# Inverting unit triangular matrices from 16x16 instead of 32x32 diagonal blocks, two chunks together, in a hybrid decoder layer

## The chip, the cores and the metric

The kernel runs on one core of one Trainium2 chip. A core has a matrix engine (PE, with its weight loads shown apart as PEld), a vector engine (DVE), an activation engine (ACT), a general engine (POOL) and an engine that issues transfers (SP). Each works through a queue of its own in a fixed order, and a transfer between on-chip memory and DRAM runs on DMA engines beside them. The metric is the device time of one execution, in microseconds (us).

## What is computed

One layer of a decoder over a prompt of 4096 tokens (width 1024), and one decoding step for 8 samples. The layer has a gated delta-rule half (4 heads of 128) and a sliding-window attention half (8 heads of 64); the change touches the first alone. Cut to that half, the reference is:

```python
h   = x * (1 + scale) + shift
p   = h @ w_in                              # one input projection
q, k, v = causal_conv(p[..., A_QKV])        # width 4, SiLU; q, k L2-normed
beta, g = sigmoid(p[..., BETA]), -exp(a_log) * softplus(p[..., DECAY] + dt_bias)

# per chunk of tokens and head, G = cumsum(g):
lower = eye + beta[:, None] * (k @ k.T) * exp(G_t - G_i)[t > i]
w_mat, u_tilde = solve(lower, [beta * exp(G) * k, beta * v])   # unit lower triangular
a_qk  = (q @ k.T) * exp(G_t - G_i)[t >= i]
# from chunk to chunk, S the state of a head:
u = u_tilde - w_mat @ S
o = (exp(G) * q) @ S + a_qk @ u
S = exp(G_last) * S + (exp(G_last - G) * k).T @ u
```

The solve needs the inverse of one unit triangular matrix per chunk and head. The kernel uses chunks of 128 tokens.

## The kernel before, in words

The program has two phases. Phase 1 (up to about 1270 us of the profile) runs the delta half; phase 2 runs the attention windows, gates and the output projection, and reads the weights that phase 1 split and stored for it. The change leaves phase 2's code alone.

Phase 1 goes over 16 supertiles of 256 tokens, two chunks `c` of 128 each, with 4 heads, so 8 triangular matrices of 128x128 per supertile. One supertile is written as:

- `front(s)`: the beta and decay products (tile `bd`, 32 small matmuls with weights `wbd`), a softplus by a polynomial in ten DVE operations (lines 101 to 108), the decays `g`, `g16`, `G`; projections into tile `pj` (12 blocks of 24 matmuls of 256 columns); the convolution on DVE (line 347); the matrices `k k^T` (tile `pga`), their decay masks (`tr<-g`), and U, the strictly triangular matrices, scaled by ACT at line 416 once a supertile; U is split into two 16-bit parts (U16). Inside it, `ahead()` loads and transposes the next supertile's x and makes its `hT`.
- `lanes(s, U)`, lines 437 to 466: the diagonal blocks of U, 32x32, are inverted by substitution on DVE. To lay them out by lanes, they go to DRAM (tile D1, 4 transfers at line 443) and come back replicated four times (LU, line 445, 512 KB). 31 steps of a multiplication (line 452) and an addition (line 454) follow, each on at most 8 x 31 columns. The result LV goes to DRAM (D2, line 456, 128 KB) and returns as diagonal blocks of VTd (4 transfers at line 461).
- `gdn_inv(c)`, once for each chunk, lines 470 to 513: on 4 matrices at a time, PE transposes VTd (line 487) and joins blocks 32 to 64 and 64 to 128. Each of the two levels is two groups of small matmuls (64 columns each), and between any two groups ACT (line 482) and DVE (line 483) take a result apart into two 16-bit halves.
- `gdn_c(s, c)`, once for each chunk: the recurrence of S with 128x128 products in 32-bit, and the output `oq`.

Beside this run the preparation of phase 2's weights (`prep`, `prep_s`), the gates' columns and, in steps, the decoding samples (`dec_a`). The framework's scheduler puts all instructions into one static queue per engine; a queue does not let later work pass one that waits. SP's queue issues all the transfers named here. Of the tiles in question U, U16, LU, LV, `vt16` and VTd have one buffer each.

Of the kernel before, what the change touches and what calls it, by code (L numbers as in the profile page):

```python
# [33 lines left out]
def body(ctx, tc, I, O, seq):  # L34
# [57 lines left out]
    D1 = [dr.tile([32, 1024], F32, name=f"D1_{i}") for i in range(2)]  # L92
    D2 = [dr.tile([32, 1024], F32, name=f"D2_{i}") for i in range(2)]
# [4 lines left out]
    def softplus_ops(t, x, out, shape, nm):  # L98
        """out = softplus(x) in SBUF tiles of one shape"""
        ab = t.tile(shape, F32, name=nm + "ab", bufs=2)  # L100
        dve.scalar_tensor_tensor(ab, x, -1.0, x, op0=ALU.mult, op1=ALU.max)
# [3 lines left out]
        dve.tensor_scalar(p, u, LOG1P[-1], None, op0=ALU.mult)  # L105
        for c in LOG1P[-2::-1]:
            dve.scalar_tensor_tensor(p, p, c, u, op0=ALU.add, op1=ALU.mult)
        dve.scalar_tensor_tensor(out, x, 0.0, p, op0=ALU.max, op1=ALU.add)

    # ================================================================ phase 1  # L110
    hpx = ctx.enter_context(ExitStack())
    hp = hpx.enter_context(tc.tile_pool(name="hp", bufs=2))
    with ExitStack() as p1:
# [40 lines left out]
        def raw():  # L154
            """a buffer for weights as they come, lent by the chunks' matrices"""
# [20 lines left out]
        # c^T, constants by channel  # L176
# [30 lines left out]
        # shift and scale: rows first, then by channel  # L207
# [24 lines left out]
        # ---- samples: h  # L232
# [9 lines left out]
        # ---- phase-1 weights  # L242
# [24 lines left out]
        XE = w1p.tile([128, 2, 4, 128], F16, name="XE")  # L267
        XZ = w1p.tile([128, 2, 4, 128], F16, name="XZ")
        V64 = w1p.tile([128, 2, 4, 64], F16, name="V64")
        VR = w1p.tile([128, 2, 4, 64], F16, name="VR")  # L270
        for t in (VTd, XE, XZ, V64, VR):
            pool.memset(t, 0.0)
# [19 lines left out]
        def front(s, hT, ahead):  # L292
            """projections, convolution, decays and the chunk's matrices"""
# [10 lines left out]
            be = sml.tile([128, 2, 4], F32, name="be")  # L304
# [5 lines left out]
            softplus_ops(sml, xd, g, [128, 2, 4], "sp")  # L310
            dve.tensor_mul(g, g, nega[:, None, :].to_broadcast([128, 2, 4]))
            dve.tensor_scalar(g, g, -30000.0, None, op0=ALU.max)
            g16 = sml.tile([128, 2, 8], F16, name="g16")
            gf = g.rearrange("p a b -> p (a b)")
            dve.tensor_copy(g16[:, 0], gf)
            dve.tensor_sub(g16[:, 1], gf, g16[:, 0])
            kqv = wk.tile([128, 8, 256], F32, name="kqv", bufs=2)
            vv = wf.tile([128, 4, 256], F32, name="vv", bufs=1)
            U = wk.tile([128, 8, 128], F32, name="U", bufs=1)
            U16 = wk.tile([128, 2, 8, 128], F16, name="U16", bufs=1)  # L320
# [35 lines left out]
            # keys  # L356
# [42 lines left out]
            # queries  # L399
# [15 lines left out]
            vt, vt16 = lanes(s, U)  # L415
# [10 lines left out]
            # values  # L426
# [8 lines left out]
            return kqv, G, sc, U16, Aqk, Kd, Vn, eGl, vt, vt16  # L435
# [984 lines left out]
```

## Time and profile before

| | us |
|---|---|
| median of 3 runs (2459.22 to 2463.24) | 2462.24 |
| span of the profiled execution | 2462.7 |
| PE busy | 2171.7 |
| DVE busy | 1942.7 |
| ACT busy | 1262.8 |
| POOL busy | 640.3 |

The profiled execution is 0.5 us above the median, so its durations can be set against the median as they are.

How the rows further down are to be read. A group row of the trace gives line, engine, operation, output tile, input tiles, shape and count, then total busy time and mean ns of one, then the engine's idle time just before, and what ended most of it; the view of one tile gives minimum, median and maximum in ns, and the times of the first and the last. A wait row gives the waiting engine, its output tile and line, what it waited for, and then total us, number of waits and the longest. A timeline row gives start and length in us; for SP the length is the time to issue.

A windows row gives the stretch and its length, then the busy us (and count) of PE, PEld, DVE, ACT and POOL, then the granted PE clock, the share of DMA engines busy and GB/s. Two kinds of stretch are told apart there. A *front stretch* runs from the scaling of U at line 416 to the first transposes of VTd at line 487, that is, through the transfers, the substitution and the transfers back. A *back stretch* runs from there to the next supertile's scaling at line 416. The recurrences lie partly in the one and partly in the other. Seven front stretches from 707.31 us on were summed, and eight back stretches from 677.36 us on. The mean of a sum row is over the stretches of that sum.

### The profile page before, as it was taken

To read this page: it belongs to the slowest core of one execution; us is meant where nothing else is said; L and a number is where in the kernel's file an instruction comes from. 1 tells how busy PE (TensorE), PEld (TensorE's weight loads), DVE (VectorE), ACT (ScalarE), POOL (GpSimd) and SP (SyncE) were. 2 spreads that over 40 slices of the span, in tenths; PEclk is the share of its full clock that TensorE was granted. 3 is DMA by queue.
4 is the path that set the end of the run, shared out by engine and by line. 5 is a ranking of instruction groups with operands and counts; after the bars stand their busy time and mean duration, and the time that the engine had idled before them with its cause. 6 is when DMAs were issued, how large, how long until landed. Compare 5 with 4: busy or idle time off the path is not lost. (4 is left out here: it accounts for less than half of the span.)

```text
span 2462.7 us, 49809 instructions
## 1 busy us (share of the span) xinstructions
PE 2171.7 (88%) x18596; PEld 1540.5 (63%) x18596; DVE 1942.7 (79%) x5348; ACT 1262.8 (51%) x3603; POOL 640.3 (26%) x669
## 2 busy tenths in 40 slices
PE   7988888878878888988899999999889888989986
PEld 4877777767766677777767677776445444444443
DVE  7678788767788877776776877776787789999997
ACT  6566555556557666545546656656323233333332
POOL 1122122202333311101100200000354555656552
PEclk8999999999899999999999999999999999999998
DMA  9232232322344221011314211110522222323231
GB/s 312 87 104 68 89 86 84 101 77 68 95 142 133 96 67 61 25 57 59 96 56 189 89 59 70 57 59 22 197 82 88 98 78 97 109 82 124 69 111 61
DMA packets 177409, 228.05 MB, mean 93 GB/s; under 512 B 65978, under 2 KB 120375, under 8 KB 171000
## 3 DMA queue, kind: packets, MB, share of 16 engines
q1 hardware_dynamic: 176696, 224.36, 28.0%
q8 instruction: 146, 2.39, 0.4%
q0 software_dynamic: 208, 0.37, 0.1%
q14 instruction: 95, 0.78, 0.1%
q10 hardware_dynamic: 264, 0.14, 0.0%
HBM read 149.88 MB, written 76.09 MB: 92 GB/s over the span
## 5 line engine op out<-in xcount | busy, mean ns | idle before, releaser
L41 PE MATMUL pj<-hT,w 128*128 128x256 f16 x4608 | 598.0, 281 | 5.9 <-ACT hT L287 2.8
L41 PEld LDWEIGHTS <-w 128*128 128x128 f16 x4800 | 459.8, 101 | 76.0 <-issue 15.7
L41 PEld LDWEIGHTS <-hT 128*128 128x128 f16 x2660 | 221.9, 99 | 146.1 <-issue 22.7
L41 PEld LDWEIGHTS <-S 128*128 128x128 f16 x1536 | 150.7, 98 | 182.2 <-issue 4.9
L41 PE MATMUL pj<-wq,hT 128*128 128x512 f16 x768 | 191.2, 381 | 1.9 <-DVE qt L826 1.9
L347 DVE SCALAR_TENSOR_TENSOR kqv<-u,cols,kqv 128x256 f32<-128x256 f32 x384 | 185.6, 490 | 7.2 <-ACT kqv L345 5.8
L452 DVE TENSOR_TENSOR lt<-LV,LU 128x60 f32<-128x60 f32 (+24 forms) x496 | 137.6, 277 | 65.4 <-DMA LU<-D 58.4
L1072 POOL TENSOR_TENSOR zt<-hT 128x512 f32<-128x512 f16 x32 | 43.2, 1351 | 496.6 <-DMA hT<-hD 496.6
L41 PE MATMUL pp<-wz,S 128*128 128x512 f16 x768 | 172.0, 382 | 0.1
L41 PE MATMUL pp<-wo,S 128*128 128x512 f16 x768 | 168.6, 379 | 1.0 <-DVE u L1107 1.0
L911 ACT ACTIVATE Sm<-Sm,nm 128x256 f32<-128x256 f32 (+1 forms) x256 | 125.5, 492 | 79.5 <-DVE nm L908 79.2
L41 PE MATMUL pp<-wz,hT 128*128 128x512 f16 x576 | 147.2, 405 | 0.0
L1072 POOL TENSOR_TENSOR zt<-zt,hT 128x512 f32<-128x512 f32 x112 | 142.8, 1280 | 6.3
L41 PE MATMUL pp<-wo,A 128*128 128x512 f16 x540 | 125.9, 389 | 11.7 <-DVE u L1105 8.9
L904 DVE CUSTOM_DVE_ANT_0 Sm<-pS,swam 128x256 f32<-128x256 f32 (+1 forms) x256 | 96.4, 415 | 38.2 <-PE tr L928 36.4
L332 POOL COPY u<-hist 128x6 f32<-128x6 f32 x96 | 24.9, 261 | 377.2 <-DVE kqv L347 104.8
L1241 POOL TENSOR_TENSOR u<-u,gateB 128x512 f32<-128x512 f32 x60 | 81.2, 1363 | 147.7 <-DVE u L1099 81.1
L454 DVE TENSOR_TENSOR LV<-LV,lt 128x60 f32<-128x60 f32 (+24 forms) x496 | 111.6, 225 | 7.1
L41 PE MATMUL pj<-wkv,hT 128*128 128x256 f16 x768 | 104.7, 273 | 0.4 <-ACT v L855 0.4
L41 PEld LDWEIGHTS <-A 128*128 128x128 f16 x540 | 53.9, 100 | 78.5 <-issue 16.8
L1135 POOL TENSOR_TENSOR x<-x,lnb 128x512 f32<-128x512 f32 (+1 forms) x62 | 84.9, 1380 | 67.5 <-ACT x L1134 67.5
L1066 ACT ACTIVATE S<-zt 128x512 f16<-128x512 f32 x64 | 40.0, 628 | 120.3 <-POOL zt L1072 120.3
(418 smaller groups left out, 5016.1 us busy)
## 6 DMA issues: line engine op xcount, KB each, us to landing
hT<-hD SPq DMA_DIRECT2D x32, 1024.0 KB
x<-in_x_prompt_dram SPq DMA_DIRECT2D x32, 512.0 KB
hD<-hT SPq DMA_DIRECT2D x16, 1024.0 KB
x<-in_x_prompt_dram SPq DMA_DIRECT2D x60, 256.0 KB
out_y_prompt_dram<-x SPq DMA_DIRECT2D x60, 256.0 KB
LU<-D SPq DMA_DIRECT2D x16, 512.0 KB
wS<-wt SPq DMA_DIRECT2D x16, 512.0 KB
oD<-oq SPq DMA_DIRECT2D x32, 256.0 KB
```

The lines of the kernel that those rows point to most:

```text
L41: pe.matmul(out, l, r, start=st, stop=sp_)
L332: pool.tensor_copy(u[:, :, 0:3], hist[:, b0:b0 + 2, :])
L347: dve.scalar_tensor_tensor(d, u[:, b2, j:j + 256], cwj(j, blk), d, op0=ALU.mult, op1=ALU.add)
L452: dve.tensor_mul(lt[:, j0:, 0:j], LV[:, j0:, j:j + 1].to_broadcast([128, n, j]), LU[:, None, 0:j, j].to_broadcast([128, n, j]))
L454: dve.tensor_add(LV[:, j0:, 0:j], LV[:, j0:, 0:j], lt[:, j0:, 0:j])
L904: dve.tensor_tensor_reduce(Sm[:, h, k0:256], pS[:, h2, k0:256], swam[:, k0:256], 0.125, -1e30, op0=ALU.add, op1=ALU.max, accum_out=mx[:, h ...
L911: act.activation(Sm[:, h, k0:256], Sm[:, h, k0:256], AF.Exp, bias=nm[:, h:h + 1], accum_out=sm_[:, h:h + 1])
L1066: act.activation(q[:, 0], src, AF.Copy)
L1072: pool.tensor_tensor(o, x, y, op=ALU.add if sgn > 0 else ALU.subtract)
L1135: (dve if last else pool).tensor_tensor(r[q][0:n], r[q][0:n], lnb[0:n, qs_], op=ALU.add)
L1241: (dve if last else pool).tensor_tensor(C, C, gateB[:, 512 * ch:512 * ch + 512], op=ALU.mult)
```

## The change

It alters four things in phase 1.

1. The diagonal blocks that DVE inverts are 16x16. U's blocks go out in 8 transfers and come back in 8; the replicated LU has 128 KB in two copies, LV 64 KB. There are 15 steps. LU and LV have two buffers, and LV's initial values are copied by POOL.
2. `gdn_inv` runs once for the 8 matrices of both chunks, and has a level 16 to 32 ahead of the two others. It has 144 products of 64 columns in place of 96 a supertile, 24 transposes in place of 16 (the last 8 of them 64x64), and splits of 512 columns. U16 has two buffers.
3. The decays are a function `decays(hT)`, called from `ahead`, so that those of supertile s+1 stand in the program inside supertile s; `be`, `g16` and `G` have three buffers.
4. Constants are loaded from ACT's queue and no longer from POOL's, `Sb` of the decoding step borrows a buffer, and the scratch memory for POOL's own transfers is made smaller.

```diff
-    D1 = [dr.tile([32, 1024], F32, name=f"D1_{i}") for i in range(2)]
+    D1 = [dr.tile([64, 256], F32, name=f"D1_{i}") for i in range(2)]
...
-        def front(s, hT, ahead):
+        def decays(hT):
             bd = tr_ps([128, 2, 16])
...
+            G = sml.tile([128, 4, 8], F32, name="G", bufs=3)
+            act.activation(G[:, 0], ps, AF.Exp)
+            act.activation(G[:, 1], ps, AF.Copy, scale=-1.0)
+            dve.tensor_scalar(G[:, 2], G[:, 0], -1.0, None, op0=ALU.mult)
+            return be, g16, G
+
+        def front(s, hT, dcy, ahead):
+            be, g16, G = dcy
...
-            for b in range(4):
-                bs = slice(32 * b, 32 * b + 32)
+            for b in range(8):
+                bs = slice(16 * b, 16 * b + 16)
                 sp.dma_start(d1v[b], U[bs, :, bs])
-            LU = w1p.tile([128, 32, 32], F32, name="LU", bufs=1)
-            sp.dma_start(LU.rearrange("p a b -> p (a b)"), d1[None].to_broadcast([4, 32, 1024]))
-            LV = w1p.tile([128, 8, 32], F32, name="LV", bufs=1)
-            dve.tensor_copy(LV.rearrange("p a b -> p (a b)"), lv0)
+            LU = w1p.tile([128, 16, 16], F32, name="LU", bufs=2)
+            sp.dma_start(LU.rearrange("p a b -> p (a b)"), d1[None].to_broadcast([2, 64, 256]))
+            LV = w1p.tile([128, 8, 16], F32, name="LV", bufs=2)
+            pool.tensor_copy(LV.rearrange("p a b -> p (a b)"), lv0)
...
-            for j in range(31, 0, -1):
-                j0 = j // 4
+            for j in range(15, 0, -1):
+                j0 = j // 2
...
-            d2w = d2.rearrange("l (j c i) -> c l j i", c=4, i=32)
+            d2w = d2.rearrange("l (j c i) -> c l j i", c=2, i=16)
             sp.dma_start(d2w, LV)
...
+            for c in range(2):
+                pb = pgi.tile([128, 4, 128], F32, name="pgi")
+                for h in range(4):
+                    pe.transpose(pb[:, h, :], vt[:, 4 * c + h, :], ident)
+                act.activation(V[:, 4 * c:4 * c + 4], pb, AF.Copy)
+            te = wk.tile([128, 2, 8, 64], F16, name="vt16", bufs=1)
+            sub([rows(te[:, z], 16) for z in range(2)], blocks(vt, 16, 0))
+            level(16, XF, te)
...
+            level(32, XE, te)
...
         def ahead(s):
             if s < NS:
-                nxt[0] = xt(s, load_x(s))
+                hT = xt(s, load_x(s))
+                nxt[:] = [hT, decays(hT)]
...
-            Vs = [gdn_inv(c, U16, vt, vt16) for c in range(2)]
+            V = gdn_inv(U16, vt)
             for c in range(2):
-                gdn_c(s, c, kqv, G, sc, Aqk, Kd, Vn, eGl, Vs[c])
+                gdn_c(s, c, kqv, G, sc, Aqk, Kd, Vn, eGl, V)
```

`level(b, XB, te)` is the new function for one level of 8 matrices: a split of V's off-diagonal half into `Vo`, 24 products with U16, a split into XB, 24 products with `Vo`, and the copies of the joined blocks into V, by ACT and DVE in turn. The scheduler's queues shift with it, at three places.

DVE, in the substitution of a supertile in the middle of phase 1, before; `spp` is the polynomial of the decays.

```order
L105 TENSOR_SCALAR spp<-spu 128x8
L452 TENSOR_TENSOR lt<-LV,LU 128x4x19
L107 SCALAR_TENSOR_TENSOR spp<-spp,spu 128x8
L454 TENSOR_TENSOR LV<-LV,lt 128x4x19
L107 SCALAR_TENSOR_TENSOR spp<-spp,spu 128x8
L452 TENSOR_TENSOR lt<-LV,LU 128x4x18
```

The same engine at the end of a substitution after; L360 is the convolution (L347 before).

```order
L360 SCALAR_TENSOR_TENSOR kqv<-u,cols,kqv 128x256
L460 TENSOR_TENSOR LV<-LV,lt 128x7x3
L360 SCALAR_TENSOR_TENSOR kqv<-u,cols,kqv 128x256
L458 TENSOR_TENSOR lt<-LV,LU 128x7x2
L360 SCALAR_TENSOR_TENSOR kqv<-u,cols,kqv 128x256
L460 TENSOR_TENSOR LV<-LV,lt 128x7x2
L458 TENSOR_TENSOR lt<-LV,LU 128x8
L460 TENSOR_TENSOR LV<-LV,lt 128x8
```

The decays' polynomial has left the substitution, whose steps stand among convolution operations alone.

DVE, in the last level of the inverse of one chunk, before; VR, V_368 (a buffer of V64) and XZ are written by splits of results.

```order
L483 TENSOR_TENSOR VR<-V,VR 64x256
L347 SCALAR_TENSOR_TENSOR vv<-u,cols,vv 128x256 x2
L483 TENSOR_TENSOR V_368<-pgi,V_368 64x256
L354 SCALAR_TENSOR_TENSOR kqv<-th,kqv 128x1024
L483 TENSOR_TENSOR XZ<-pgi,XZ 64x4x64
```

The same level after, for both chunks.

```order
L483 TENSOR_TENSOR VR<-V,VR 64x512
L483 TENSOR_TENSOR V_369<-pgi,V_369 64x512
L105 TENSOR_SCALAR spp<-spu 128x8
L107 SCALAR_TENSOR_TENSOR spp<-spp,spu 128x8
L367 SCALAR_TENSOR_TENSOR kqv<-th,kqv 128x1024
L107 SCALAR_TENSOR_TENSOR spp<-spp,spu 128x8
L360 SCALAR_TENSOR_TENSOR vv<-u,cols,vv 128x256
L107 SCALAR_TENSOR_TENSOR spp<-spp,spu 128x8
L360 SCALAR_TENSOR_TENSOR vv<-u,cols,vv 128x256
L483 TENSOR_TENSOR XZ<-pgi,XZ 64x8x64
```

Between the splits of V64 and XZ, where one other operation stood, there are seven; the polynomial is among them.

SP, the transfers of one supertile's lanes, before (`D_1_87` is D1, `D_1_89` is D2).

```order
L443 DMA D_1_87<-U 32x8x32 x3
L546 DMA oD<-oq 128x512
L443 DMA D_1_87<-U 32x8x32
L445 DMA LU<-D_1_87 128x1x1024
L546 DMA oD<-oq 128x512
L456 DMA D_1_89<-LV 4x256x32
L461 DMA VTd<-D_1_89 32x8x32 x4
```

The transfers of one supertile's lanes after.

```order
L572 DMA oD<-oq 128x512 x2
L449 DMA D_1_87<-U 16x8x16 x8
L451 DMA LU<-D_1_87 128x1x256
L462 DMA D_1_89<-LV 2x512x16
L467 DMA VTd<-D_1_89 16x8x16 x8
```

The outputs of the recurrence (`oq`) stand ahead of U's transfers and no longer among them.

## Rows read from the trace of the kernel before

**Rows 1.** Page, part 1: busy time, share, instructions of each engine, whole span.

```profile
PE 2171.7 (88%) x18596; PEld 1540.5 (63%) x18596; DVE 1942.7 (79%) x5348; ACT 1262.8 (51%) x3603; POOL 640.3 (26%) x669
```

**Rows 2.** ACT's scaling of U, line 416, once a supertile: first and last start.

```profile
L416 ACT ACTIVATE U<-U x16: 1042/1057/1058, 94.5 to 1212.4; 128x1024 f16<-128x1024 f32 x16
```

**Rows 3.** Windows, busy us: a front stretch, seven front summed, eight back summed.

```profile
931.60:978.20 46.60, 39.95 (x386) 34.91 (x385) 36.25 (x147) 27.65 (x99) 6.34 (x12) 1.00 0.16 40
sum 353.59, PE 285.62 PEld 248.14 DVE 266.75 ACT 198.75 POOL 76.74; mean PE 40.80 PEld 35.45 DVE 38.11 ACT 28.39 POOL 10.96
sum 181.45, PE 167.46 PEld 136.55 DVE 146.84 ACT 119.87 POOL 26.86; mean PE 20.93 PEld 17.07 DVE 18.36 ACT 14.98 POOL 3.36
```

**Rows 4.** Waits of PE, 115 to 1245 us: total us, times, longest.

```profile
PE tr L41 <- DVE g L315: 20.7, 7, 6.5
PE pgi L487 <- DMA VTd<-D: 16.3, 11, 2.7
```

**Rows 5.** Waits of DVE, the same stretch.

```profile
DVE lt L452 <- DMA LU<-D: 58.4, 15, 6.9
DVE LV L447 <- DMA D<-LV: 42.8, 13, 4.8
```

**Rows 6.** DVE groups by shape, 115 to 1245 us: busy us, mean ns.

```profile
L465 DVE TENSOR_TENSOR vt<-VTd,vt 128x512 f16<-128x512 f32 x15 | 10.4, 691 | 7.7 <-ACT vt L464 7.6
L483 DVE TENSOR_TENSOR XE<-pgi,XE 128x256 f16<-128x256 f32 x30 | 12.6, 421 | 1.2 <-ACT XE L482 0.8
L347 DVE SCALAR_TENSOR_TENSOR kqv<-u,cols,kqv 128x256 f32<-128x256 f32 x354 | 171.8, 491 | 6.4 <-ACT kqv L345 5.1
```

**Rows 7.** Tile LV: the substitution, ns minimum/median/maximum.

```profile
L452 DVE TENSOR_TENSOR lt<-LV,LU x496: 136/252/2237, 111.3 to 1245.8; 128x60 f32<-128x60 f32 x16, 128x28 f32<-128x28 f32 x12, 128x66 f32<-128x66 f32 x11, 128x48 f32<-128x48 f32 x10
L454 DVE TENSOR_TENSOR LV<-LV,lt x496: 170/214/2124, 111.8 to 1246.0; 128x60 f32<-128x60 f32 x16, 128x28 f32<-128x28 f32 x12, 128x66 f32<-128x66 f32 x11, 128x48 f32<-128x48 f32 x10
```

**Rows 8.** Timeline of SP in one supertile: start us, us it took to issue.

```profile
617.02 1.31 SPq L443 DMA_DIRECT2D D<-U  x3
619.59 0.96 SPq L443 DMA_DIRECT2D D<-U  x1
623.48 0.54 SPq L445 DMA_DIRECT2D LU<-D  x1
668.08 0.58 SPq L456 DMA_DIRECT2D D<-LV  x1
672.88 1.83 SPq L461 DMA_DIRECT2D VTd<-D  x4
```

**Rows 9.** Timeline of DVE, same supertile: first and last substitution steps.

```profile
632.72 0.21 DVE L452 TENSOR_TENSOR lt<-LV,LU 128x31 f32<-128x31 f32 x1 [4.70 <-DMA LU<-D]
666.34 0.21 DVE L452 TENSOR_TENSOR lt<-LV,LU 128x28 f32<-128x28 f32 x1
667.87 0.18 DVE L454 TENSOR_TENSOR LV<-LV,lt 128x8 f32<-128x8 f32 x1
```

**Rows 10.** Timeline of PE, two places: start us, us, count.

```profile
604.46 0.51 PE L41 MATMUL pgi<-vt,U 128*128 128x64 f16 x12
604.81 1.11 PE L41 MATMUL pga<-kqv 128*128 128x256 f32 x4
668.96 3.77 PE L41 MATMUL pj<-hT,w 128*128 128x256 f16 x33
677.36 0.63 PE L487 MATMUL pgi<-cf,VTd 128*128 128x128 f32 x4
...
1197.94 0.60 PE L487 MATMUL pgi<-cf,VTd 128*128 128x128 f32 x4
1205.10 0.22 PE L41 MATMUL pgi<-VR,XZ 128*128 128x64 f16 x2
1212.52 0.91 PE L41 MATMUL pgi<-S,kqv 128*128 128x128 f32 x6
1226.24 1.06 PE L41 MATMUL pgi<-ut,Aqk 128*128 128x128 f32 x8
```

More of the change, by code (lines that the diff above doesn't have):

```diff
@@ L266, in body @@
         VTd = w1p.tile([128, 8, 128], F32, name="VTd")
[L267 to L271, printed above, removed]
+        XF = w1p.tile([128, 2, 8, 128], F16, name="XF")
+        XE = w1p.tile([128, 2, 8, 128], F16, name="XE")
+        XZ = w1p.tile([128, 2, 8, 128], F16, name="XZ")
+        V64 = w1p.tile([128, 2, 8, 64], F16, name="V64")
+        VR = w1p.tile([128, 2, 8, 64], F16, name="VR")
+        for t in (VTd, XF, XE, XZ, V64, VR):
             pool.memset(t, 0.0)
@@ L483, in sub @@
                 dve.tensor_sub(dst[1], src, dst[0])
-            pb = pgi.tile([128, 4, 128], F32, name="pgi")
-            for h in range(4):
-                pe.transpose(pb[:, h, :], vt[:, m0 + h, :], ident)
-            act.activation(V, pb, AF.Copy)
-            vo = V.rearrange("p h (a b) -> p h a b", b=64)[:, :, :, 32:64]
-            sub([Vo[:, 0], Vo[:, 1]], vo)
-            px = pgi.tile([128, 4, 2, 32], F32, name="pgi")
-            for h in range(4):
-                mm3(px[:, h], lambda a: U16[:, a, m0 + h, :], lambda b: vt16[:, b, m0 + h])
@@ L502, in gdn_inv, with bank @@
[L502 to L511 removed]
+            def bank():
+                return pgi.tile([128, 8, 64], F32, name="pgi")
@@ new lines, in blocks, with rows, level @@
+            def blocks(t, b, o):
+                return t.rearrange("p m (a b) -> p (m a) b", b=2 * b)[:, :, o:o + b]
+            def rows(t, b):
+                return t.rearrange("p m (a b) -> p (m a) b", b=b)
+            def level(b, XB, te):
+                vo = wk.tile([128, 2, 8, 64], F16, name="Vo", bufs=1)
+                sub([rows(vo[:, z], b) for z in range(2)], blocks(V, b, b))
+                px = bank()
+                mm3(px, U16, te)
+                sub([blocks(XB[:, z], b, 0) for z in range(2)], rows(px, b))
+                pv = bank()
+                mm3(pv, XB, vo)
+                for n, a in enumerate(range(64 // b)):
+                    r0 = 2 * b * a
+                    dst, src = V[r0:r0 + b, :, r0 + b:r0 + 2 * b], pv[r0:r0 + b, :, a * b:a * b + b]
+                    if n % 2 == 0:
+                        act.activation(dst, src, AF.Copy)
+                    else:
+                        dve.tensor_copy(dst, src)
@@ new lines, in gdn_inv @@
+            for c in range(2):
+                cs = slice(4 * c, 4 * c + 4)
+                pt = pgi.tile([128, 4, 128], F32, name="pgi")
+                for h in range(4):
+                    pe.transpose(pt[:, h, :], V[:, 4 * c + h, :], ident)
+                sub([rows(te[:, z, cs], 32) for z in range(2)], blocks(pt, 32, 0))
+            level(32, XE, te)
+            sub([VR[64:128, z] for z in range(2)], V[64:128, :, 64:128])
+            pt = bank()
+            for m in range(8):
+                pe.transpose(pt[0:64, m, :], V[0:64, m, 0:64], ident[0:64, 0:64])
@@ L512, in gdn_inv @@
+            sub([V64[0:64, z] for z in range(2)], pt[0:64])
+            p2 = bank()
+            mm3(p2, U16, V64)
+            sub([XZ[64:128, z, :, 0:64] for z in range(2)], p2[64:128])
+            p3 = bank()
+            mm3(p3, XZ, VR)
             act.activation(V[0:64, :, 64:128], p3[0:64], AF.Copy)
@@ L532, in gdn_c @@
             for h in range(4):
[L533 removed]
+                mm(pw[:, h, :], V[:, m0 + h, :], r[:, h, :])
             ut = wk.tile([128, 4, 128], F32, name="ut", bufs=1)
@@ L743, in body @@
         load_bd()
+        nxt.append(decays(nxt[0]))
         for g in (4, 5, 6, 7):
```

108 lines of the change are left out of this document (40 added, 68 removed).

## The prediction

> **What bounds the kernel now.** I read the engines' busy times first [rows 1]: PE is busy for 2171.7 of 2462.7 us, so over the whole span little is left to win by filling PE. But the change touches phase 1 alone, and there the share has to be read by stretch. The scaling of U comes once a supertile, 16 times from 94.5 to 1212.4 us [rows 2], so a supertile takes 1117.9 / 15 = 74.5 us. The windows then tell where PE is idle [rows 3]. A front stretch (U out, LU in, substitution, LV out, VTd in) lasts 353.59 / 7 = 50.5 us, and PE works 40.8 of them: 9.7 idle. A back stretch lasts 181.45 / 8 = 22.7 us, and PE works 20.9: 1.8 idle. A period of these is 73.2 us (the early supertiles, with gates and decoding beside them, are longer), PE's own work in it 61.7 us, its idle time 11.5.
>
> What ends the idle time [rows 4]: PE waits 20.7 us in all for the decays' g, 16.3 for VTd. DVE waits 58.4 us for LU and 42.8 for the old LV to leave before it may be filled anew [rows 5]; since DVE's queue lets nothing pass, these waits hold up what PE reads next too. So the front stretch is set by the chain of transfers and substitution, and PE's 40.8 us of work there, nearly as long, covers most of it. Shortening that chain pays only as far as PE's work in the stretch is shortened or moved.
>
> **The chain, step by step, in one heavy supertile** [rows 8, 9, 10]. U's first transfer 617.02 to LU's issue 623.48: 6.46 (the four issues take some .45 each; from the last one's end at 620.55, landing takes 2.9). LU to the first step 632.72: 9.24. Steps until 668.05: 35.3, with much other DVE work between. LV's issue to VTd's first 672.88: 4.8. Four issues 1.83. Landing until the first transpose at 677.36: 2.65. Sum 60.3 in this long one.
>
> **The change, part 1: transfers and substitution.** Eight issues in place of four, at .44 (1.31 / 3): 3.5; landing 2.9 as before. LU has 128 KB in place of 512: no row shows it, it lies between 2.9 (a landing with little data) and 9.24; I take 4.8, the time of the 128 KB that LV now takes, the nearest row in size. Of the 31 steps the 15 narrowest stay. The four last pairs took 668.05 - 666.34 = 1.71 [rows 9], .43 each, so 15 take 6.5; the medians of .252 and .214 [rows 7] would give 7.0. The queue after the change has one split and six convolution operations between them: 0.69 + 6 x 0.49 = 3.6 [rows 6]. I take 10, between 6.5 and, by the heavy supertile's pace, 35.3 x 15 / 31 = 17. LV's way out: 4.8, although it has half the bytes. Eight issues of VTd at .46: 3.7. Landing 2.65. Front chain: 3.5 + 2.9 + 4.8 + 10 + 4.8 + 3.7 + 2.65 = **32.4 us**, bounds 27 (LU 2.9, steps 6.5) and 44 (9.24, 17). LV's first values are copied by POOL into a second buffer, so the 42.8 us of DVE waiting go; I cost the copy at nothing, since POOL is busy 26% [rows 1] and the buffer is free a supertile ahead. Uncovered it costs under 1 us a supertile.
>
> **Part 2: what PE does meanwhile.** The chain is shorter only if PE's work leaves the front, and the new order moves it: of some 230 projections in a front stretch 52 go to the back, with all 32 beta and decay products, some 11 transposes of x, and 24 products of the recurrence (32-bit). Prices [rows 10]: projection 3.77 / 33 = .114, so 5.9; 32-bit products 0.60 / 4 = .15, so 1.7 and 3.6; the 32 small ones at some .025, 0.8. Sum 12.0: PE has 40.8 - 12.0 = 28.8 us of work in a chain of 32.4, so the chain still ends last, by 3.6.
>
> **Part 3: the back stretch.** 12.0 us arrive. New work: 48 more products of 64 columns at (604.81 - 604.46) / 12 = .029, 1.4 us, and 8 more transposes at .15 or less, 1.2 us. At the back's present ratio of length to work, 22.7 / 20.9 = 1.085: 22.7 + 14.6 x 1.085 = 38.5. Against it stands the chain through the inverse, which is now one for both chunks: one chunk's took 1205.10 - 1197.94 = 7.2 with two levels [rows 10], so three levels of both some 7.2 x 2 x 1.5 = 21.6, and both recurrences behind it 1212.52 to 1227.3, 14.8. That is 36.4, just under PE's 38.5. A split is twice as wide (512 columns took .691, 256 .421 [rows 6]). I add 0.7, one such split that PE finds no other work for: **39.2 us**, bounds 36 and 44.
>
> **Part 4: decays ahead, loads.** PE's 20.7 us for g, 1.3 a supertile [rows 4], lie in the idle time that the front sum replaces, so nothing is added for them: DVE's polynomial now stands beside the inverse's splits, where the back sum's bounds hold it. The constants' loads, the decoding step's borrowed buffer and phase 2: no change, within 3 us in all.
>
> **Sum.** 32.4 + 39.2 = 71.6 for 73.2, -1.6 us a supertile, times 16: -26. From 2462.7 that is **2437 us**.
>
> **Rivals.** *R1, PE is the bound.* The two stretches run into each other (two buffers of LU, LV and U16 allow it), and nothing but PE's work counts: 61.7 + 2.6 = 64.3, with 2 us of its idle time left 66.3; -6.9 x 16 = -110, **2352 us**. For it: VTd's waits are 16.3 us in all, 1 us a supertile, so PE mostly finds other work [rows 4]. Against it: U has one buffer, and PE's waits in the back grow with the longer chain.
>
> *R2, slower: the inverse's hand-offs set the back.* The joined inverse has no second chunk to run beside it. It has some 15 hand-offs from PE to ACT and DVE and back, and each split stands behind convolution operations of .49 and polynomial steps. At 0.5 us more for each hand-off the chain is 36.4 + 7.5 = 43.9, the period 32.4 + 43.9 = 76.3, +3.1 x 16 = +50: **2512 us**. It decides from a back of 73.2 - 32.4 = 40.8, or 0.3 us a hand-off. For it: seven DVE operations stand between two splits of the chain that one parted before. Against it: today the splits wait hardly at all, 1.2 us in 30 [rows 6].
>
> *R3, slower: the passes through DRAM do not get shorter.* LU and LV have half as many outer pieces (two, not four). If each piece goes at a pace of its own, fewer bytes don't help as far. Taking 2.65 as the fixed part, LU's pieces of 128 KB took 9.24 - 2.65 = 6.6, so 64 KB take 3.3, and LU 5.95. LV's pieces had 256 rows in 4.8 - 2.65 = 2.15; they now have 512 half as long, so up to 4.3, and the pass 6.95. The front is 1.15 + 2.15 longer, 35.7, the period 74.9, +1.7 x 16 = +27: **2490 us**. For it: the 512 KB of LU take only twice as long as the 128 KB of LV, so time goes not by bytes alone [rows 8, 9]. Against it: 2.65 as the fixed time is an estimate from one landing of 32 KB transfers.
>
> The Trainium skill speaks for R3, and against this change: "DMA: Bandwidth & Descriptors", section Rules for kernel authors, says that an outermost dimension of fewer than 16, a leading broadcast of c copies above all, confines a transfer to at most c engines; LU and LV would go from 4 engines to 2. No row shows which engines a transfer used, so the trace neither confirms nor denies it; by it the sum would be R3's.
>
> **How the numbers follow.** Forecast .50, R1 .17, R3 .18, R2 .15. The measurement tells about 0.2% from no change, here 5 us. Of the forecast's share .43 lies below 2457, .05 within and .02 above (a substitution at 17 us would do it). R1 is faster; of R3 .03 and of R2 .02 lie within, the rest above. Faster .60, same .10, slower .30. The range reaches from near R1 to beyond R3, 2360 to 2500: it leaves out half of R1 and most of R2's upper half, .18.
>
> **What would show it.** The front window at some 32 us (33.6 or longer with its LU above 5.5 would be R3), with PE at 29 us of work; DVE's waits for LU near a half of 58.4, and those for the old LV gone; 15 pairs of steps in 10 us. The back window at 39 with PE idle under 3; idle over 5 there, released by splits, would be R2. Period of U's scaling 73 in the mean for 74.5. I am wrong if PE's waits within the inverse exceed 4 us a supertile, if work said to move stays in the front, or if phase 2, which no line of the change touches, moves by more than 3 us.

## The result, and the profile after

The changed kernel takes 2497.48 us (median of 4 runs, 2492.07 to 2505.32) beside 2462.74 of the kernel before in the same session: ratio 1.0136, 95% interval 1.0112 to 1.0159, so it is 1.4% slower, 35 us. The forecast was 2437. Of the rivals, R3 named 2490.

The busy times of the whole span, the row that answers [rows 1]:

```profile
PE 2198.5 (88%) x19492; PEld 1570.6 (63%) x19492; DVE 1860.5 (75%) x4788; ACT 1284.4 (51%) x3619; POOL 625.7 (25%) x681
```

PE works 26.8 us longer, DVE 82 us less. The scaling of U, the row that answers [rows 2], as the view of the tile gives it (in the code this line is ACT's copy of U into its 16-bit part U16, in both kernels; as a mark for the stretches it serves as well):

```profile
L422 ACT ACTIVATE U<-U x16: 1046/1057/1088, 97.1 to 1237.1; 128x1024 f16<-128x1024 f32 x16
```

From first to last it is 1140.0 us for 1117.9: 22.1 of the 35 us. Of these the twelve periods in the middle make 17.4, the first two 16.4, and the last is 11.7 shorter; why those at the two ends differ so was not looked into. 2.7 lie ahead of the first scaling and the rest behind the last. The first projection with `wq` (phase 2) starts 33.7 us later than before, and the end of the span is 33.7 later. Phase 2 itself has not moved.

Up to the copy `hr<-tr` near the end of phase 1 (line 777 before, 805 after), one window of each kernel (length, PE busy, PEld, DVE, ACT, POOL, granted clock, DMA share, GB/s), before:

```profile
0.00:1228.20 1228.20, 1042.23 (x9935) 881.97 (x9936) 945.08 (x3009) 732.23 (x2270) 240.60 (x349) 0.94 0.31 95
```

and after:

```profile
0.00:1259.90 1259.90, 1064.17 (x10769) 909.97 (x10770) 877.95 (x2500) 754.65 (x2293) 230.69 (x362) 0.94 0.29 86
```

Phase 1 is 31.7 us longer up to there; PE is busy 21.9 of them and idle 9.8. So the time that DVE gave back (67 us in this stretch) bought PE nothing.

To set stretch against stretch, the same twelve periods were taken in every kernel, from the third scaling of U to the fifteenth (the prediction had seven front and eight back stretches of mixed supertiles, which [rows 3] shows). Fronts first, backs second, summed; the kernel before:

```profile
sum 626.07, PE 509.06 PEld 444.13 DVE 479.97 ACT 363.61 POOL 157.68; mean PE 42.42 PEld 37.01 DVE 40.00 ACT 30.30 POOL 13.14
sum 280.91, PE 263.65 PEld 216.19 DVE 224.00 ACT 180.02 POOL 31.19; mean PE 21.97 PEld 18.02 DVE 18.67 ACT 15.00 POOL 2.60
```

The changed kernel:

```profile
sum 430.67, PE 324.71 PEld 282.17 DVE 274.35 ACT 220.21 POOL 81.16; mean PE 27.06 PEld 23.51 DVE 22.86 ACT 18.35 POOL 6.76
sum 493.70, PE 467.96 PEld 405.84 DVE 370.78 ACT 342.77 POOL 100.79; mean PE 39.00 PEld 33.82 DVE 30.90 ACT 28.56 POOL 8.40
```

A period has 75.6 us before and 77.0 after. The front fell from 52.2 to 35.9 us, as meant, and PE's work there from 42.4 to 27.1; its idle time in the front was 9.8 and is 8.8. The back grew from 23.4 to 41.1, with 39.0 of work. PE's waits, the rows that answer [rows 4]:

```profile
PE tr L393 <- DVE kqv L367: 77.0, 14, 8.1
PE pgi L515 <- DMA VTd<-D: 25.0, 8, 5.4
PE tr L437 <- DVE vv L367: 10.7, 5, 8.9
```

The waits for g are gone. The longest now has 77.0 us, in 14 waits, where it had 13.9 us in 4: the transposes of the keys wait for the last step of the keys' SiLU on DVE (L367, L354 before). One supertile in the middle shows why. SP (start, time to issue):

```profile
640.46 4.32 SPq L449 DMA_DIRECT2D D<-U  x8
646.32 0.50 SPq L451 DMA_DIRECT2D LU<-D  x1
664.72 0.52 SPq L462 DMA_DIRECT2D D<-LV  x1
672.31 3.64 SPq L467 DMA_DIRECT2D VTd<-D  x8
```

DVE, first and last step of the substitution and what follows:

```profile
651.46 0.18 DVE L458 TENSOR_TENSOR lt<-LV,LU 128x15 f32<-128x15 f32 x1 [1.49 <-DMA LU<-D]
664.52 0.17 DVE L460 TENSOR_TENSOR LV<-LV,lt 128x8 f32<-128x8 f32 x1
665.84 2.31 DVE L367 SCALAR_TENSOR_TENSOR kqv<-th,kqv 128x1024 f32<-128x1024 f32 x1 [1.15 <-ACT th L366]
```

PE, up to the first transposes of VTd:

```profile
651.51 9.88 PE L41 MATMUL pj<-hT,w 128*128 128x256 f16 x89
661.79 0.28 PE L41 MATMUL pga<-c,g 128*128 128x128 f16 x2
668.20 1.12 PE L393 MATMUL tr<-cf,kqv 128*128 128x128 f32 x4 [6.14 <-DVE kqv L367]
...
677.68 1.04 PE L515 MATMUL pgi<-cf,VTd 128*128 128x128 f32 x8
```

LU took 5.14 us to its first step, the 15 steps 13.2, with 12 convolution operations and a piece of the decoding step between them, and the pass of LV, from its issue to VTd's first, 7.59. PE has done its projections and masks by 662.1 and then waits 6.14 us for L367, which stands behind the substitution in DVE's queue; it does the little work that stands next and is at VTd's transposes at 677.68.

DVE stands still in the same place, before its half of the split of VTd:

```profile
678.03 0.69 DVE L483 TENSOR_TENSOR vt<-VTd,vt 128x512 f16<-128x512 f32 x1 [7.51 <-ACT vt L482]
```

It waits 7.51 us, until VTd has landed and ACT has made the other half, and nothing in its queue can pass. From 95 to 1263 us these waits have 9.4 us in the kernel before and 79.0 in the changed one:

```profile
DVE vt L465 <- ACT vt L464: 9.4, 10, 2.4
DVE vt L483 <- ACT vt L482: 79.0, 13, 8.6
```

DVE's waits for LU did fall as the prediction had it, from 58.4 to 30.6 us, and those for the old LV are gone.

Over the 16 supertiles the medians are (each from the rows of SP, DVE and PE as above):

| | before | forecast | after |
|---|---|---|---|
| issuing U's transfers | 2.7 | 3.5 | 3.8 |
| landing, to LU's issue | 2.1 | 2.9 | 1.3 |
| LU's issue to first step | 9.4 | 4.8 | 5.6 |
| first step to last | 27.8 | 10 | 11.8 |
| LV's pass through DRAM | 4.77 | 4.8 | 7.54 |
| issuing VTd's transfers | 1.8 | 3.7 | 3.6 |
| landing, to the transposes | 1.6 | 2.65 | 1.7 |
| sum | 50.2 | 32.4 | 35.4 |

LV's pass has half the bytes of before and takes 2.8 us longer, in every supertile (7.52 to 7.70, but for the first). R3 had priced the front at 35.7, and the prediction's sign for it, a front of 33.6 us or longer with LU above 5.5, is met.

### The profile page after: what moved, and what is told of

Read it like the earlier page. It is cut to its first block, busy times and chain, and to the rows that moved or that the text cites. A ratio compares the mean times of both kernels' runs of the same rounds, so it can differ in the third digit from the quotient of the medians.

```text
span 2496.4 us, 51161 instructions
## 1 busy us (share of the span) xinstructions
PE 2198.5 (88%) x19492; PEld 1570.6 (63%) x19492; DVE 1860.5 (75%) x4788; ACT 1284.4 (51%) x3619; POOL 625.7 (25%) x681
## 5 line engine op out<-in xcount | busy, mean ns | idle before, releaser
L41 PEld LDWEIGHTS <-w 128*128 128x128 f16 x4800 | 451.3, 100 | 77.0 <-issue 17.0
L41 PEld LDWEIGHTS <-hT 128*128 128x128 f16 x2660 | 228.4, 99 | 164.6 <-issue 19.7
L360 DVE SCALAR_TENSOR_TENSOR kqv<-u,cols,kqv 128x256 f32<-128x256 f32 x384 | 179.0, 493 | 28.6 <-ACT kqv L358 27.1
L41 PE MATMUL pj<-wq,hT 128*128 128x512 f16 x768 | 182.6, 382 | 0.0
L41 PE MATMUL pp<-wo,A 128*128 128x512 f16 x540 | 127.9, 393 | 12.7 <-DVE u L1133 9.4
L932 DVE CUSTOM_DVE_ANT_0 Sm<-pS,swam 128x256 f32<-128x256 f32 (+1 forms) x256 | 95.0, 415 | 33.7 <-PE tr L956 33.2
L41 PEld LDWEIGHTS <-A 128*128 128x128 f16 x540 | 54.2, 101 | 81.6 <-issue 19.6
L393 PE MATMUL tr<-cf,kqv 128*128 128x128 f32 x128 | 28.1, 350 | 81.9 <-DVE kqv L367 77.0
L1162 ACT ACTIVATE x<-x,rs 128x512 f32<-128x512 f32 (+1 forms) x62 | 42.8, 715 | 106.5 <-DVE x L1161 103.4
```

The source lines that it names most:

```text
L41: pe.matmul(out, l, r, start=st, stop=sp_)
L360: dve.scalar_tensor_tensor(d, u[:, b2, j:j + 256], cwj(j, blk), d, op0=ALU.mult, op1=ALU.add)
L393: pe.transpose(pk[:, h, :], kqv[:, 4 + h, c * 128:(c + 1) * 128], ident)
L932: dve.tensor_tensor_reduce(Sm[:, h, k0:256], pS[:, h2, k0:256], swam[:, k0:256], 0.125, -1e30, op0=ALU.add, op1=ALU.max, accum_out=mx[:, h ...
L1162: act.activation(r[q][0:n], r[q][0:n], AF.Copy, scale=rs[0:n, 1:2])
```

## The experiments

Two theories stood first. *Pieces*: the time goes into LV's and LU's passes, which are slow because the transfers have two outer pieces. *Order*: the queues' order is what counts; PE waits for the keys' SiLU behind the substitution, and LV's pass lies beside that. A third, *work*: what was added is the third level.

Every kernel's queues are ordered anew when it is built, so unless it is said otherwise two kernels differ in their order too. In the sessions of these runs the kernel before took 2462.7 to 2468.2 us, so where two runs of different sessions are compared, the difference of their ratios to the kernel before, taken of 2462.7 us, is given beside that of their times.

**LV's pass alone (a1_lv).** Two transfers, each with the 64 lanes outermost:

```diff
-            sp.dma_start(d2w, LV)
+            for z in range(2):
+                sp.dma_start(d2w[z], LV[64 * z:64 * z + 64])
```

> The changed kernel, but LV is written to DRAM by two transfers of 64 partitions each, with the 64 lanes as their outermost dimension, in place of one with an outermost dimension of two. Theory 'pieces' (the pass of LV through DRAM is slow since the write has two outer pieces, and this pass ends the front stretch): the pass, from LV's issue to VTd's first issue, falls from 7.5 us to some 3.5; the front stretch falls from 35.5 to 32; the kernel from 2497 to about 2450. Theory 'order' (PE's idle time in the front is its wait for the keys' SiLU, 77 us in all, which stands behind the substitution on DVE, and the pass is beside it): the pass may fall, but only PE's waits for VTd, 25 us in all, can go: 2475 to 2497.

Measured: 2435.88 us, ratio 0.9883 (0.9861 to 0.9904) to the kernel before. 62 us are back. SP of one supertile:

```profile
623.67 0.54 SPq L451 DMA_DIRECT2D LU<-D  x1
642.41 1.21 SPq L463 DMA_DIRECT2D D<-LV  x2
645.20 4.21 SPq L468 DMA_DIRECT2D VTd<-D  x8
```

The pass is 2.79 us from first issue to VTd, 2.81 in the median for 7.54. 4.73 us less in each of 16 supertiles are 76 us, and 62 came. PE's wait that 'order' took for the cause is as large as ever:

```profile
PE tr L393 <- DVE kqv L367: 74.2, 14, 8.7
```

but PE's waits for VTd, 25 us, are gone, and DVE's waits at VTd's split fell from 79.0 to 44.0 us:

```profile
DVE vt L484 <- ACT vt L483: 44.0, 15, 6.6
```

The two theories parted at 2475; the time is far below it. So the pass does not lie beside the chain, as 'order' had it, and PE's list of waits alone had shown too little: a VTd that comes late also holds DVE's queue, and with it all that stands behind. PE has as much work in a front as in the changed kernel (27.0 us for 27.1) and is idle 6.0 us there for 8.8. Two things stay open: the queues are ordered anew, so not each of the 62 us is shown to be the transfer's, and whether this write is faster by being two transfers or by having its lanes outermost was not told apart.

**LU too (a3_lvlu)**, by two transfers of 64 partitions (`for z in range(2): sp.dma_start(LU[64 * z:64 * z + 64]..., d1)`):

> As a1_lv, and LU too is read by two transfers of 64 partitions, one for each copy. Theory 'pieces': LU falls from 5.6 us to about 4, LV's pass from 7.5 to 3.5, the front to 30.5, the kernel to about 2430. Theory 'order': the substitution starts 1.6 us earlier and PE's waits for the keys' SiLU fall by that, 25 us in all, on top of at most 25 for VTd: 2450 to 2480.

Measured: 2391.6 us, 0.97 (0.9678 to 0.9722). LU's time is 4.4 for 5.6; the waits for L367 fall from 74 to 52 us. More than either theory gave.

**LU by its outermost dimension alone (a7_outer).** One transfer, as in the changed kernel, same bytes and rows; the lanes are numbered so that a lane's two copies are neighbours:

```diff
-            sp.dma_start(LU.rearrange("p a b -> p (a b)"), d1[None].to_broadcast([2, 64, 256]))
+            sp.dma_start(LU.rearrange("p a b -> p (a b)"), d1[:, None].to_broadcast([64, 2, 256]))
...
-                sp.dma_start(d2w[z], LV[64 * z:64 * z + 64])
+                sp.dma_start(d2w[z], LV[z::2])
...
-            lane[p, jj, 2 * jj + p // 64] = 1.0
+            lane[p, jj, 2 * jj + p % 2] = 1.0
```

> The changed kernel with LV written by two transfers as in a1_lv, and LU read by one transfer as in the changed kernel, of the same bytes and the same rows of 1 KB; only its outermost dimension is 64 (each lane's row twice in a row) in place of 2, for which the lanes are numbered the other way round. Theory 'pieces': LU falls from 5.6 us to 4 or less, as with two transfers, and the kernel comes to 2392 or, with one issue less, 2385. If it was the number of transfers in flight that helped and not the outermost dimension: as a1_lv, 2436.

Measured: 2403.87 us, 0.974 (0.9725 to 0.9754). This kernel and a1_lv have the same instructions in the same order on every engine; the pattern of one transfer is all that differs, with the lanes' numbers (LV's pass, whose two writes follow them, takes 2.79 us for 2.81). LU's first step came 5.38 us after the issue there (623.67, above, and DVE's row)

```profile
629.05 0.18 DVE L458 TENSOR_TENSOR lt<-LV,LU 128x15 f32<-128x15 f32 x1 [2.57 <-DMA LU<-D]
```

and here 2.56 us after it, with no wait for LU before it (SP, then DVE):

```profile
612.15 0.55 SPq L451 DMA_DIRECT2D LU<-D  x1
```

```profile
614.71 0.18 DVE L458 TENSOR_TENSOR lt<-LV,LU 128x15 f32<-128x15 f32 x1
```

In the median it is 3.8 for 5.5, 1.7 us a supertile, and the kernel gains 32 us, 2.0 a supertile. Of the 2.0, 1.3 are idle time of PE; 0.7 are its work, the same instructions at a granted clock of 0.963 for 0.960 over the span. DVE's waits for LU fall from 29.7 us to 0.4, and PE's for L367 by 20 us:

```profile
PE tr L393 <- DVE kqv L367: 53.8, 14, 6.6
PE pgi L516 <- DMA VTd<-D: 2.3, 2, 1.4
```

So the outermost dimension, not the number of transfers, made LU slow. The Trainium skill, "DMA: Bandwidth & Descriptors", section Rules for kernel authors, says just this of a leading broadcast of few copies (it confines the transfer to at most as many engines as there are copies), and the trace agrees in effect: 128 KB in 5.5 us with 2 outermost, 3.8 with 64. No row shows which engine carried a packet, but the kept traces hold the start, length and size of each. In the twelve supertiles LU's 128 packets of 1 KB run 2.1 at a time in the mean in a1_lv, never more than 4, and the last ends 4.7 to 5.9 us after the issue. In a7_outer up to 15 to 21 run at once, and the last ends within 2.4 us in ten of the twelve, at 4.0 at the latest. LV's 1024 packets of 64 bytes show the same: at most 5 at once in the changed kernel, the last ending 6.3 to 6.4 us after the issue; up to 19 to 21 at once in a1_lv, the last ending at 2.3. Why a7_outer is 12 us slower than a3_lvlu, whose LU is the slower one, was not tried; their queues are ordered differently.

**The kernel before with the same repair**, by four transfers each (b1_lvlu):

> The kernel before, with LV written and LU read by four transfers each, of 32 partitions, outermost dimension 32. Theory 'pieces': LU falls from 9.4 us to 4.3, LV's pass from 4.8 to 3.2, DVE's waits for LU from 58 us to 10, and the kernel from 2463 to some 2410. Theory 'order': VTd's waits of PE are 16 us in all, so at most 2445; the DVE waits for LU have other work behind them and cost nothing.

Measured: 2382.56 us, 0.9673 (0.9647 to 0.9699). The time fell by more than was expected, but LU's first step comes 11.9 us after the first issue, not 4.3, and LV's pass takes 4.3, not 3.2. DVE, which waited 58.4 us for LU [rows 5], does not wait for it at all here: it comes to the first step late, with other work ahead of it in its queue. So in this kernel and the next, issue to first step is not the transfer's time. And LU alone (b4_lu):

> The kernel before with LU read by four transfers, LV still written by one with an outermost dimension of 4. b1_lvlu had both and came to 2383. If LU's time is what counted in the kernel before (DVE's waits for LU, 58 us, and all that stands behind them in its queue): 2380 to 2395. If LV's pass, which fell only from 4.8 to 4.3 us there, counted: 2440 to 2463.

Measured: 2405.04 us, 0.9743 (0.972 to 0.9766): some 60 us are LU's, 22 LV's (63 and 17 by the ratios), each with the order that goes with it, so both readings of the expectation were too pure. With LU by one transfer, outermost dimension 32 (b7_outer):

> The kernel before with LV written by four transfers and LU read by one whose outermost dimension is 32 in place of 4, lanes numbered the other way round. Theory 'pieces': LU is as fast as by four transfers or faster, since three issues of .45 us are gone: 2370 to 2383. If the number of transfers counts: LU 9.4 us as before, and the kernel at some 2430.

Measured: 2363.89 us, 0.9578 (0.9562 to 0.9594), the fastest here: 4.2% below the kernel before and, by the ratios, 5.5% below the changed one. The 512 KB of LU in one supertile (SP, then DVE):

```profile
583.46 0.54 SPq L445 DMA_DIRECT2D LU<-D  x1
```

```profile
588.92 0.21 DVE L452 TENSOR_TENSOR lt<-LV,LU 128x31 f32<-128x31 f32 x1 [2.01 <-DMA LU<-D]
```

5.46 us, for 9.24 in [rows 8, 9]. DVE's waits, which were 58.4 and 42.8 us in [rows 5]:

```profile
DVE lt L452 <- DMA LU<-D: 6.1, 5, 2.0
DVE LV L447 <- DMA D<-LV: 9.3, 8, 2.3
```

So the old blocks had the same fault in LU, hidden in DVE's waits, and with the fault mended in both, 32x32 blocks (2364) beat 16x16 (2392).

**What the new level costs (n1_nolevel).** The level 16 to 32 is left out:

```diff
-            te = wk.tile([128, 2, 8, 64], F16, name="vt16", bufs=1)
-            sub([rows(te[:, z], 16) for z in range(2)], blocks(vt, 16, 0))
-            level(16, XF, te)
```

> The changed kernel without the level 16 to 32 (its 48 products and its splits are left out, so the blocks between are not inverted; transposes stay). It prices the new level. Theory 'work': PE's busy time falls by some 37 us (48 products at .029 to .045 a supertile) and the kernel by about as much, to 2455 to 2465. If the hand-offs of the level count (four, some 1.2 us each, 5 us a supertile): 2410 to 2420. If the back hides it: 2485 to 2497.

Measured: 2448.93 us, 0.9926 (0.9906 to 0.9945). The level costs 48 us, 3.0 a supertile (52 by the ratios; 2.5 a period in the twelve). PE's busy time there falls by 1.8 a period, so it is more than work, and far less than four hand-offs of 1.2 us; the time lies between the ranges that were expected.

**Joined or by chunk (c1_chunk).** The inverse once for each chunk, on 4 matrices, all three levels:

```diff
-            V = gdn_inv(U16, vt)
+            Vs = [gdn_inv(c, U16, vt) for c in range(2)]
```

> The changed kernel, but with the inverse run once for each chunk, on four matrices, as before the change, with the third level and the splits of 256 columns that go with it. If the joint chain (no second chunk to run beside it) is what made the back stretch 41 us: back 38 to 39, the kernel 2450 to 2465. If joining helps (half as many hand-offs, splits of twice the width at 1.6 times the price): DVE and ACT get 5 us a supertile more to do, 2520 to 2560.

Measured: 2530.14 us, 1.025 (1.0231 to 1.027). Joining the chunks gains 33 us here (28 by the ratios). With 32x32 blocks and two levels, joined, on b7_outer's transfers (c2_joint32):

> b7_outer with the inverse of the changed kernel but for its new level: 32x32 blocks, 31 steps, both chunks' 8 matrices together, levels 32 and 64, decays made ahead. If joining saves what c1_chunk lost (33 us with three levels, so some 20 with two): 2340 to 2350. If joining only helped to hide the new level's hand-offs: as b7_outer, 2364, or above.

Measured: 2364.64 us, 0.9587 (0.9568 to 0.9605): no gain beside b7_outer. Here joining, with the decays ahead and the second buffers that came with it, pays only with the third level. This kernel differs from a7_outer in the size of the blocks and the third level, and but for that only in LU's one buffer, LV's four writes for two and the order: by the ratios it is 38 us faster. So, the order aside, with the transfers mended it is the 16x16 blocks and the level they need that cost.

**Decays (a4_dec).** Back at the start of each front (`be, g16, G = decays(hT)` in `front`):

> The changed kernel with its decays made at the start of each supertile's front again, as before. If the polynomial beside the inverse's splits is what slows the back stretch (41 us measured, 39 forecast): back 39 or less, 2470 to 2485. If making them ahead is worth what PE waited for g before (20.7 us): 2515 to 2520. Theory 'work' (what was added is the third level on PE, 25 us of busy time, and decays don't matter): 2490 to 2505.

Measured: 2497.0 us, 1.0121 (1.0087 to 1.0154). No difference: PE waits 62.8 us for g, and those for L367 are gone. With the polynomial out of the inverse the back takes 40.7 us, for 41.1.

**What the substitution is worth (g1_nosteps).** All but the last of the 15 steps left out (`for j in range(1, 0, -1)`):

> The changed kernel with 14 of the 15 substitution steps left out (the 16x16 blocks are not inverted); all transfers stay. It prices what is left of the substitution, 11.8 us from the first step to the last. If the chain through transfers and steps ends the front stretch (35.5 us, PE at work in 27): the chain falls to some 25 us, PE's 27 set the front, and the kernel gains 14 x 8 = 110 us, to 2385. If the substitution was already hidden and PE waits for the convolution itself: 2460 to 2497.

Measured: 2485.42 us, 1.0065 (1.0043 to 1.0087): 12 us (17 by the ratios) for the 110 expected. The twelve fronts and backs:

```profile
sum 302.62, PE 210.79 PEld 183.50 DVE 150.97 ACT 129.83 POOL 48.88; mean PE 17.57 PEld 15.29 DVE 12.58 ACT 10.82 POOL 4.07
sum 618.31, PE 578.82 PEld 497.42 DVE 439.94 ACT 436.76 POOL 131.39; mean PE 48.23 PEld 41.45 DVE 36.66 ACT 36.40 POOL 10.95
```

The front did fall, to 25.2 us, but PE's work in it fell as well, to 17.6, and its idle time is still 7.7. What PE does in a supertile (start, us):

```profile
644.31 8.02 PE L41 MATMUL pj<-hT,w 128*128 128x256 f16 x72
659.38 1.94 PE L515 MATMUL pgi<-cf,VTd 128*128 128x128 f32 x8 [7.05 <-DMA VTd<-D]
...
662.77 0.31 PE L41 MATMUL pga<-cb 128*128 128x128 bf16 x1
664.97 0.61 PE L393 MATMUL tr<-cf,kqv 128*128 128x128 f32 x4
```

The decay masks and the keys' transposes, which stood ahead of VTd's transposes, now stand behind them; so PE is through by 652.3 and waits 7.05 us for VTd, 104.9 us in all:

```profile
PE pgi L515 <- DMA VTd<-D: 104.9, 15, 9.0
```

The order is written before the run. With the chain shorter by steps, it puts less work in front of VTd, and the time that the transfers take is left idle as before. The same steps left out beside the fast transfers (g2_nosteps):

> a7_outer (fast transfers) with 14 of the 15 substitution steps left out; the 16x16 blocks are not inverted. g1_nosteps left the same steps out beside the slow transfers and gained 12 us of the 110 expected; PE's idle time in a front stretch stayed near 8 us while the stretch fell from 35.5 to 26. Theory 'allowance' (the static order gives PE as much work in the front as the chain is taken to need, steps counted, so PE's idle time there is what the transfers take beyond that, whatever the steps): idle stays near the 5 us of a7_outer, and the kernel gains 0 to 20 us, 2385 to 2404. Theory 'chain' (the front's idle is chain less work, and in g1 only the slow transfers held the chain above the work): the chain falls to 18 us, idle to 1 or 2, the kernel to 2340 to 2355.

Measured: 2377.94 us, 0.964 (0.9624 to 0.9656), 26 us below a7_outer. The windows:

```profile
sum 235.74, PE 218.28 PEld 190.12 DVE 156.81 ACT 129.15 POOL 52.70; mean PE 18.19 PEld 15.84 DVE 13.07 ACT 10.76 POOL 4.39
sum 602.00, PE 555.66 PEld 476.82 DVE 433.15 ACT 433.37 POOL 127.86; mean PE 46.31 PEld 39.73 DVE 36.10 ACT 36.11 POOL 10.65
```

Between the theories, outside both their ranges: the gain is nearer 'allowance' (0 to 20) than 'chain' (50 to 60), but the front's idle time fell to 1.5, as 'chain' had it, and the back's rose to 3.9.

Over the twelve periods, in us (LU, LV's pass and steps are medians; lengths and idle from windows as shown, those of the other kernels from the same view; the column LU is the time from issue to first step):

| kernel | LU | LV's pass | steps | front, PE idle in it | back, PE idle in it | period |
|---|---|---|---|---|---|---|
| before | 9.4 | 4.8 | 27.8 | 52.2, 9.8 | 23.4, 1.4 | 75.6 |
| after | 5.6 | 7.5 | 11.8 | 35.9, 8.8 | 41.1, 2.1 | 77.0 |
| a4_dec | 5.7 | 7.5 | 12.3 | 36.6, 8.6 | 40.7, 1.9 | 77.3 |
| g1_nosteps | 5.6 | 7.6 | 0.7 | 25.2, 7.7 | 51.5, 3.3 | 76.7 |
| n1_nolevel | 5.8 | 7.6 | 11.5 | 35.7, 8.7 | 38.8, 1.6 | 74.5 |
| c1_chunk | 5.6 | 7.6 | 12.3 | 36.1, 9.1 | 42.3, 2.8 | 78.4 |
| a1_lv | 5.5 | 2.8 | 12.7 | 33.0, 6.0 | 40.3, 2.5 | 73.3 |
| a7_outer | 3.8 | 2.8 | 12.6 | 30.8, 4.6 | 40.5, 2.5 | 71.3 |
| g2_nosteps | 3.6 | 3.5 | 0.7 | 19.6, 1.5 | 50.2, 3.9 | 69.8 |
| a3_lvlu | 4.4 | 2.8 | 12.6 | 31.6, 4.2 | 38.9, 2.2 | 70.5 |
| b7_outer | 5.3 | 4.1 | 29.7 | 48.5, 5.1 | 19.9, 1.3 | 68.4 |
| c2_joint32 | 5.5 | 4.3 | 27.1 | 47.1, 5.7 | 22.1, 1.5 | 69.1 |
| b4_lu | 11.2 | 4.8 | 28.2 | 50.7, 6.8 | 20.2, 1.5 | 70.9 |
| b1_lvlu | 11.9 | 4.3 | 28.8 | 50.5, 4.7 | 16.7, 1.2 | 67.3 |

Read downwards, PE's idle time in the front goes with LU plus LV's pass (13 to 14 us: 7.7 to 9.8 idle; 6.6 to 9.8 us: 4.2 to 6.0), and not with the steps, of which there were 28 us or 0.7. Three fall out of the line: g2_nosteps, and b4_lu and b1_lvlu, where DVE does not wait for LU and the column is no transfer's time. The twelve periods are not the whole either: b1_lvlu has the shortest of them and is 19 us slower than b7_outer, since its first two periods and its last take 51 us more.

## Why the prediction was wrong, point by point

- **LV's pass "4.8, although it has half the bytes"**: the step that failed. It was 7.54. The nearest row was nearest in bytes, and bytes did not set the time: the write went from four outer pieces to two, with twice the rows in each. R3 had this at 6.95, with a chance of .18, and its front of 35.7 is close to the measured 35.4. a1_lv, with the pass at 2.81, is 62 us faster, enough to turn the sign, though its queues are ordered anew. In proportion, the 2.7 us by which the term was too small would be some 36 us of the 60 between forecast and result (an estimate from 62 us for 4.73).
- **LU, 4.8**: 5.6; R3 had 5.95. a7_outer shows the cause, and by its 32 us for 1.7 the 0.8 would be some 15 us (an estimate again).
- **Substitution, 10**: 11.8 in the median, between 8.8 and 14.4 in the twelve periods' light and heavy supertiles. The order shown had six convolution operations among the steps; the twelve supertiles have 4 to 12.
- **PE's work**: 28.8 in the front was forecast, 27.1 came; in the back 35.5, and 39.0 came. More moved than was counted: in the twelve periods 59 projections for 52, and of the recurrence all of some 47 products that stood in a front, for 24. The back's base was too small, since the sample of eight stretches had 20.9 where the twelve periods have 22.0. On equal stretches the forecast added 2.6 us of work to a period, and 64.4 became 66.1.
- **Idle time "the chain still ends last, by 3.6"**: the second step that failed. It was taken as chain less work, and should have gone from 11.5 a period (11.2 on the twelve) to 7.3. It stayed at 11.0. These 4 us, times 16, are 64 us; PE's work, 0.9 less a period than forecast, gives back 15, and the rest of the 60 us between forecast and result lies outside the twelve periods. With the transfers mended, a7_outer comes near the forecast's idle time: front 30.8 and back 40.5, 71.3 in sum, idle 7.2; its windows, fronts and backs:

```profile
sum 369.38, PE 313.68 PEld 274.06 DVE 280.63 ACT 221.79 POOL 93.25; mean PE 26.14 PEld 22.84 DVE 23.39 ACT 18.48 POOL 7.77
sum 485.93, PE 455.74 PEld 393.21 DVE 374.50 ACT 337.97 POOL 103.53; mean PE 37.98 PEld 32.77 DVE 31.21 ACT 28.16 POOL 8.63
```

  That the sum comes to the forecast's 71.6 is luck: the forecast stood on periods of 73.2, and on the twelve, of 75.6, it is 74.0; and a7_outer's transfers are shorter than forecast (LU 3.8, LV 2.8, for 4.8 each). a1_lv, whose 8.3 us for the two are already under the forecast's 9.6, is still idle 8.4 us a period. And g1_nosteps shows that the reasoning was incomplete: a shorter chain on DVE gave PE nothing, since the written order took work out of the front along with it.
- **R1**: against it stood that U has one buffer; PE stayed idle 11 us a period.
- **R2**: the back came to 41.1, just beyond the 40.8 from which R2 was to decide, but by PE's work; idle is 2.1 there, and c1_chunk shows that joining saves some 30 us. The operations between two splits cost little: after the first supertile a4_dec has two to five there and no polynomial, for three to ten, and its back is 0.4 us shorter.
- **Part 3's new level**: priced at 3.5 us in all, of which eight transposes have 1.3. n1_nolevel keeps the transposes, so its 3.0 stands against 2.2: somewhat dearer than priced.
- **The other signs**: a period of the scaling takes 76.0 us in the mean, for the 73 forecast.
- **Part 4, decays, loads, phase 2 at nothing**: right (a4_dec; phase 2, from the first projection with `wq` to the end, 1232.8 us before and 1232.9 after).

What is left open: why g2_nosteps has less idle time in the front and more in the back than a7_outer, and how much of the gaps between kernels whose queues are ordered anew (a3_lvlu and a7_outer, b1_lvlu and b7_outer) is the order's. Only a1_lv and a7_outer have one order and are free of it.

## What to carry to other kernels

Before a transfer is costed by its bytes, look at the outermost dimension of both its sides: a small tile replicated by a leading broadcast of 2 or 4, or written by column groups, can take as long as one four times its size (5.5 us for 128 KB with 2 outermost, 5.3 for 512 KB with 32). Numbering the lanes so that the lanes are outermost mends the read with one transfer as before; the write took one transfer for each column group. Where queues are ordered ahead of the run, shortening a stage that the order counts can move PE's work elsewhere and bring little (17 and 25 us, by the ratios, for 11 us in each of 16 supertiles), while the same order with one faster transfer gained all of it and more (32 us for 1.7 us in each). And a change that trades one engine's work for another's should be tried with the transfers beside it mended on both sides: here the repair was worth 104 us to the old blocks and 107 to the new, and with the best of each side by side the change itself still costs 30 (all by the ratios).

## What the runs showed of the hardware

- A write of 64 KB from 128 partitions to DRAM as two outer pieces of 512 rows of 64 bytes took 7.54 us up to the next issue (a spread of 0.2 over all supertiles but the first), its packets running at most 5 at once; as two transfers of 64 lanes each, with the same rows, 2.81 with both issues, and up to 19 to 21 packets at once. 128 KB as four pieces of 256 rows of 128 bytes took 4.77.
- A replicating read took, from its issue to its first use, 9.4 us for 512 KB with 4 outermost and 5.3 with 32; for 128 KB, 5.5 with 2 and 3.8 with 64. The times with 32 and 64 are upper bounds, since DVE mostly did not wait for the read there; in the same supertile of a1_lv and a7_outer it was 5.38 and, at most, 2.56. With 4 and 2 outermost its packets ran 3.8 and 2.1 at a time in the mean.
- Issuing one of these transfers cost SP .45 to .6 us: the four of VTd took up 1.8 us of the queue before, the four of LV 2.5 in b7_outer; LU in one transfer with the lanes outermost took .54, as with 4 outermost.
- PE did the same instructions in 1.9 us less of busy time a period in a7_outer than in the changed kernel (64.1 for 66.1), where the granted clock of the span was 0.963 for 0.952, so less idle time went with a higher clock. a1_lv and a7_outer, with one order, had 64.9 and 64.1 at 0.960 and 0.963.
